# Six u blocks made from x before the norm, three side by side, with 1/rms multiplied on in their eviction

## The chip, the cores and the metric

The kernel runs on one core of one Trainium2 chip. The metric is device time in microseconds, the median of several runs. The engines are named as in the profile: PE (TensorE, matmuls; PEld are its weight loads), DVE (VectorE), ACT (ScalarE), POOL (GpSimd) and SP (SyncE, which here only issues DMAs). Each engine works through its own list of instructions in order, and waits for the others by semaphores.

## The reference, cut to what matters

T = 512 tokens, model width D = 1024. The program is one mixer block followed by two layers of another block; the change touches only the start of the mixer block.

```python
h = rms_norm(x, g_norm[l])                # x / sqrt(mean(x*x) + 1e-6) * g
z = h @ w_in[l]
q, k, v, fl, gf, u, gs, qm, gm, gl = split_cols(z)
log_f = log_sigmoid(fl + b_forget[l])     # 12 heads
y_fox = forgetting_attention(q, k, v, log_f)
y_s5 = s5_ssm(u, lam_re, lam_im, log_step, b_re, ...)   # u is 512 x 768
```

Since 1/rms is one number per token, `(x*g/rms) @ W` equals `((x*g) @ W)/rms`, the factor being put on column by column of the product.

## The kernel before

Activations lie feature by token: x is eight tiles of 128x512, `x[0]` to `x[7]`. A float32 matmul is made of three passes on values split in two, a high part and the rest: `mm3` (L115) issues `wh` by `h` (L117), `wh` by `l` (L118) and `wl` by `h` (L119). So each activation tile is split into h (ACT, L222) and l (DVE, L230), and each strip of weights (128x1024, 512 KB) is fetched by an SP DMA (`fetch`, L72 to L78), cast to `wh` on ACT (L93) and its rest `wl` made by DVE or, for each odd strip, by POOL (L96). A strip is two tiles of 128x512 and holds the weights of one block of 128 output features. `get` (L99) splits strips some time ahead of their use and fetches further ones.

The order of instructions on each engine is made at build time by the scheduler of the framework, from data dependences, a priority, and the kernel's own hints: `add_manual_dep` with `AFTER` (L44) orders an instruction behind another for the scheduler alone; on the chip there is no wait for it.

`block1` (L1473) begins: x comes in sixteen half tiles, ACT squares them and DVE sums the squares (`sq_acc`, L183 and L184). `norm` and `head` (L573) work by halves of the tokens: the sum over features on PE (`sumcols`, L190), mean and eps on DVE (`nv`, L208), the power -1/2 on POOL (`nr`, L210), the broadcast by PE (`bcast`, L197); then per tile `hu` = x times g times 1/rms on DVE (L562), its cast h on ACT and its rest l on DVE. With that, `head` makes the first two of six u blocks by halves (128x256, L593, L594, L597: first the passes with h, then those with l). Four more blocks come as a strip (L117 to L119). `upost` (L1497) evicts each block: an ACT copy with permuted columns to `us` (L1500), a DMA to a buffer `ud`, and four DMAs back as `u4` for the S5 stage. PSUM holds three buffers of the kind `mm` that blocks go to in turn.

Beside the head lie three things that nobody needs at once. `s5_setup` (L1124) makes the constants of the S5 stage: some hundred DVE steps on tiles of 128x24, among them two exponentials (`exact_exp`, L1091), with an ACT sine in between. `forget_load` makes the padded weights `flh` and `fll` of the forget projection (POOL memsets, L1350 and L1351, then an ACT cast and a DVE difference). `load16` and `s5_load` issue DMAs of constants. Behind the u blocks PE does the forget projection (24 matmuls of 512 columns, `pmm` from `h` and `flh`) and then fv, the v product of the forgetting attention (96 matmuls of 256 columns, L133 to L135), then its q and k.

Of the kernel before, what the change touches and what calls it, by code (L numbers as in the profile page):

```python
# [9 lines left out]
F32 = mybir.dt.float32  # L10
F32R = mybir.dt.float32r
BF16 = mybir.dt.bfloat16
I32 = mybir.dt.int32
AF = mybir.ActivationFunctionType
ALU = mybir.AluOpType
# [3 lines left out]
D = 1024  # L19
# [4 lines left out]
def f32(t):  # L24
    return t.bitcast(F32)
# [1043 lines left out]
class Blk1(Blk2):  # L1069
# [21 lines left out]
    def exact_exp(self, out, x):  # L1091

        k, r, q = self.small(), self.small(), self.small()
        xc = self.small()
        self.ts(xc, x, -150.0, 88.7, ALU.max, ALU.min)
        self.ts(k, xc, 1.4426950408889634, MAGIC)
        self.nc.vector.tensor_scalar(out=k, in0=k, scalar1=-MAGIC, scalar2=None, op0=ALU.add)
        self.stt(r, k, -0.693359375, xc, ALU.mult, ALU.add)
        self.stt(r, k, 2.12194440054690583e-4, r, ALU.mult, ALU.add)
        c = [1.0 / math.factorial(i) for i in range(9)]  # L1100
        self.nc.vector.tensor_scalar(out=q, in0=r, scalar1=c[8], scalar2=None, op0=ALU.mult)
        for i in range(7, 0, -1):
            self.stt(q, q, c[i], r, ALU.add, ALU.mult)
        self.nc.vector.tensor_scalar(out=q, in0=q, scalar1=1.0, scalar2=None, op0=ALU.add)
        ka, kb = self.small(), self.small()
        self.ts(ka, k, -126.0, 127.0, ALU.max, ALU.min)
        self.tt(kb, k, ka, ALU.subtract)
        for kk in (ka, kb):
            b = self.small(I32)
            self.ts(b, kk, 127.0, 8388608.0, ALU.add, ALU.mult)  # L1110
            self.tt(q, q, b.bitcast(F32), ALU.mult)
        self.nc.vector.tensor_copy(out, q)
# [360 lines left out]
    def block1(self):  # L1473
        nc, b = self.nc, self.base
        cst = self.t(b, [128, 1], F32, "hpi")
        nc.vector.memset(cst, 1.5707963267948966)
        self.halfpi = cst
        self.bmh = self.t(b, [128, 24], F32, "bmh")
        nc.vector.tensor_scalar(out=self.bmh, in0=self.col("b_merge", 0, 24), scalar1=0.5, scalar2=None, op0=ALU.mult)
        self.bgh = self.t(b, [128, 6], F32, "bgh")  # L1480
        nc.vector.tensor_scalar(out=self.bgh, in0=self.col("b_glu", 0, 6), scalar1=0.5, scalar2=None, op0=ALU.mult)
        x = [self.u(name="x") for _ in range(8)]
        with self.tc.high_priority():
            for hf in range(2):
                for j in range(8):
                    if 8 * hf + j == self.F0:
                        self.fetch(0)
                    nc.sync.dma_start(out=self.half(x[j], hf), in_=self.half(self.a["x"][:, j, :], hf))
        for hf in range(2):
            for j in range(8):  # L1490
                self.sq_acc(self.half(x[j], hf), j, slice(256 * hf, 256 * hf + 256))
        h = self.new_h()
        norm = self.norm(x, self.col("g_norm", 0, 8), None, h)
        u = [None] * 6
        self.y5 = [None] * 6

        def upost(j):  # L1497
            def f(pm):
                t = self.u(name="us")
                nc.scalar.copy(t.rearrange("p (i b) -> p b i", i=4), pm.rearrange("p (b i) -> p b i", i=4))  # L1500
                nc.sync.dma_start(out=self.ud[j], in_=t)
                u[j] = self.u(name="u4")
                for i in range(4):
                    nc.sync.dma_start(out=u[j][32 * i:32 * i + 32].rearrange("p (q b) -> p q b", q=4),
                                      in_=self.ud[j].rearrange("(q c) (i b) -> i c q b", q=4, i=4)[i])
            return f
        self.head(["u"] * 2, h, [upost(j) for j in range(2)],
                  norm, self.half, True)
        del x, norm
        fl = self.forget_load()  # L1510
        self.s5_load()
        self.load16()
        self.merge(self.strip("u", h, 8, [upost(j) for j in range(2, 6)]), [])
        merged = []
        ge, ges = [], ([], [])
        hm = self.fox(h, u, ge, ges, merged, fl)
        self.memory(h, hm, merged)
        return self.s5_out(h, ge, ges, merged)
# [535 lines left out]
```

## Time and profile before

| what | value |
|---|---|
| median of 3 runs | 2462.0 us (2461.26 to 2466.11) |
| profiled execution, its own time | 2459.34 us |
| its span in the trace | 2457.6 us |
| PE / DVE / ACT / POOL busy | 94% / 63% / 43% / 36% |
| DMA | 265.37 MB, mean 108 GB/s |

The span is the time from the first to the last instruction of the profiled execution; 1.7 us lie around it. A busy share is an average over stages with different limits, so the rows of the head below are read by stretch and engine. In a row of a timeline, the bracket at the end tells how long the engine was idle ahead of it and what ended that.

### The profile page before, as it was taken

The numbers are of one execution on the slowest core, as the hardware profiler recorded it, in microseconds if no ns is written. First come the engines' busy times: TensorE is split into PE (matmuls) and PEld (weight loads), VectorE is DVE, ScalarE is ACT, GpSimd is POOL, SyncE is SP. The second block draws the span as 40 slices with busy tenths as digits, with TensorE's granted clock in tenths as the row PEclk, the third lists the DMA queues.
The fourth block names the chain that finished last, engine by engine and source line by source line (L and its number), as shares of the span: only waits on it lengthen the run. The fifth ranks groups of instructions, "written<-read, shape, count | busy, mean of one in ns | idle before, by whom it ended". The sixth has DMA issues, their size and how long they took to land.

```text
span 2457.6 us, 33152 instructions
## 1 busy us (share of the span) xinstructions
PE 2322.2 (94%) x12138; PEld 1938.8 (79%) x12138; DVE 1538.6 (63%) x2573; ACT 1064.0 (43%) x1995; POOL 887.5 (36%) x810
## 2 busy tenths in 40 slices
PE   6999989989999889998999999998999899999999
PEld 5877768877888767787888888897778788888888
DVE  7567787657899788658278674257874746422222
ACT  4345543443333336643444324343565344533422
POOL 2445446635222264225132223126531523123212
PEclk9999999999999999999999999998999999999999
DMA  4311123312676321122137563232212224223222
GB/s 158 104 44 52 56 75 101 112 43 84 233 270 226 124 83 43 60 77 79 61 129 259 201 217 120 77 138 73 77 36 69 77 69 138 71 101 112 89 92 86
DMA packets 105620, 265.37 MB, mean 108 GB/s; under 512 B 13664, under 2 KB 23408, under 8 KB 105456
## 3 DMA queue, kind: packets, MB, share of 16 engines
q1 hardware_dynamic: 104304, 261.47, 31.5%
q8 instruction: 96, 1.57, 0.3%
q10 hardware_dynamic: 1152, 1.77, 0.2%
q14 instruction: 68, 0.56, 0.1%
HBM read 244.69 MB, written 9.44 MB: 103 GB/s over the span
## 4 chain that ended last, share of the span: by engine, by line
PE 63%; DVE 11%; issue 4%; ACT 3%; POOL 2%; DMA 1%; SPq 1%; DVEq 0%; POOLq 0%; ACTq 0%
PE pmm L117 17%; PE pmm L118 17%; PE pmm L119 17%; PE ps L320 3%; DVE wl L96 1%; DVE adacc L514 1%; DMA xs<-xg 1%; PE ppv L411 1%; PE ppv L410 1%; PE ppv L409 1%; DVE l L232 1%; PE pmm L134 1%; PE pmm L135 1%; PE pmm L133 1%; DVE xs L636 1%
## 5 line engine op out<-in xcount | busy, mean ns | idle before, releaser
L96 POOL TENSOR_TENSOR wl<-wr,wh 128x512 fp32r<-128x512 f32 x346 | 480.8, 1409 | 1122.6 <-ACT wh L93 968.0
L117 PE MATMUL pmm<-h,wh 128*128 128x512 f32 (+1 forms) x2112 | 824.1, 391 | 5.7 <-ACT wh L93 3.2
L119 PE MATMUL pmm<-h,wl 128*128 128x512 f32 (+1 forms) x2112 | 821.2, 389 | 2.1 <-POOL wl L96 1.8
L118 PE MATMUL pmm<-l,wh 128*128 128x512 f32 (+1 forms) x2112 | 819.5, 388 | 0.0
L119 PEld LDWEIGHTS pmm<-h,wl 128*128 128x128 f32 x2112 | 399.1, 189 | 85.7 <-POOL wl L96 4.3
L117 PEld LDWEIGHTS pmm<-h,wh 128*128 128x128 f32 x2112 | 399.4, 189 | 84.7 <-ACT wh L93 4.7
L118 PEld LDWEIGHTS pmm<-l,wh 128*128 128x128 f32 x2112 | 399.6, 189 | 77.3 <-DVE l L230 0.4
L93 ACT CAST wh<-wr 128x512 fp32r<-128x512 f32 (+1 forms) x692 | 385.1, 610 | 136.8 <-DMA wr<-in_w 118.8
L96 DVE TENSOR_TENSOR wl<-wr,wh 128x512 fp32r<-128x512 f32 x346 | 278.8, 836 | 30.3 <-ACT wh L93 26.9
L392 DVE TENSOR_TENSOR pl<-pe,ph 128x512 fp32r<-128x512 f32 (+4 forms) x168 | 121.4, 731 | 149.8 <-ACT ph L390 144.7
L230 DVE TENSOR_TENSOR l<-r,h 128x512 fp32r<-128x512 f32 x64 | 46.5, 726 | 220.9 <-ACT h L222 216.8
L971 DVE SCALAR_TENSOR_TENSOR x<-pmm,ada,x 128x512 f32<-128x512 f32 (+1 forms) x88 | 59.9, 682 | 180.5 <-PE pmm L119 180.0
L320 PE MATMUL ps<-qk,qk 128*128 128x512 f32 (+4 forms) x416 | 142.9, 381 | 24.6 <-POOL qk L683 7.4
L514 DVE SCALAR_TENSOR_TENSOR adacc<-adw,cact,adacc 128x512 f32<-128x512 f32 x168 | 156.5, 932 | 3.2
L994 ACT ACTIVATE r<-pmm 128x512 f32<-128x512 f32 x62 | 37.1, 598 | 257.1 <-PE pmm L119 257.1
L388 ACT ACTIVATE pe<-ps 128x512 f32<-128x512 f32 (+4 forms) x168 | 84.6, 503 | 102.8 <-PE ps L320 102.4
L320 PEld LDWEIGHTS ps<-qk,qk 128*128 128x128 f32 x416 | 81.0, 199 | 51.7 <-POOL qk L683 13.3
L117 PE MATMUL pmm<-yh,wh 128*128 128x512 f32 (+1 forms) x244 | 91.2, 377 | 5.8 <-ACT yh L1419 3.7
L632 POOL TENSOR_TENSOR qv<-qv,mhalf 128x8 f32<-128x8 f32 x34 | 62.9, 1852 | 86.6 <-DVE qv L631 83.1
L119 PE MATMUL pmm<-yh,wl 128*128 128x512 f32 (+1 forms) x244 | 90.7, 373 | 1.7 <-DVE wl L96 0.9
L390 ACT CAST ph<-pe 128x512 fp32r<-128x512 f32 (+4 forms) x168 | 88.8, 529 | 7.8 <-PE ppv L410 1.5
L118 PE MATMUL pmm<-yl,wh 128*128 128x512 f32 (+1 forms) x244 | 90.6, 372 | 0.3 <-DVE yl L1089 0.3
(386 smaller groups left out, 3993.2 us busy)
## 6 DMA issues: line engine op xcount, KB each, us to landing
wr<-in_w SPq DMA_DIRECT2D x324, 512.0 KB
adw<-in_wada SPq DMA_DIRECT2D x192, 256.0 KB
xs<-xg SPq DMA_DIRECT2D x136, 64.0 KB
wr<-in_w SPq DMA_DIRECT2D x22, 384.0 KB
xd<-x SPq DMA_DIRECT2D x16, 256.0 KB
x<-xd SPq DMA_DIRECT2D x16, 256.0 KB
x<-in_x SPq DMA_DIRECT2D x16, 128.0 KB
x<-in_x SPq DMA_DIRECT2D x8, 256.0 KB
```

The source lines that it names most:

```text
L93: ins = self.nc.scalar.copy(h[:, 0:m], r[:, c:c + m])
L96: eng.tensor_tensor(out=l[:, 0:m], in0=r[:, c:c + m], in1=f32(h)[:, 0:m], op=ALU.subtract)
L117: mm(out, wh, ah, start=start, stop=False)
L118: mm(out, wh, al, start=False, stop=False)
L119: self.pe = mm(out, wl, ah, start=False, stop=stop).ins.name
L320: mm(outs[i] if len(r.shape) == 2 else outs[i].rearrange("p (r i) -> p r i", r=r.shape[1]), w, r, start=first and i == 0, stop=last and i ...
L388: nc.scalar.activation(out=e[:, w], in_=pt[:, w], func=AF.Exp)
L390: nc.scalar.copy(ph[:, w], e[:, w])
L392: nc.vector.tensor_tensor(out=pl[:, w], in0=e[:, w], in1=f32(ph)[:, w], op=ALU.subtract)
L514: nc.vector.scalar_tensor_tensor(out=acc, in0=w, scalar=cc, in1=acc, op0=ALU.mult, op1=ALU.add)
L632: nc.gpsimd.tensor_tensor(out=v, in0=v, in1=self.mhalf, op=ALU.pow)
L971: nc.vector.scalar_tensor_tensor(out=x[j][:, s], in0=pm[:, s], scalar=ada[:, c + j:c + j + 1], in1=x[j][:, s], op0=ALU.mult, op1=ALU.add)
```

## The change

x now comes in eight whole tiles, with strips 0 to 2 between the first of them. For each tile ACT makes `rh` = x times g (L1495) and DVE the rest `rl` (line of `stt`, L1089); the squares are summed as before, whole tiles. Three u blocks are made side by side from `rh` and `rl`: for each of the eight tiles, nine matmuls. The sums of squares are turned to 1/rms inside the last tile's turn (`nv` on DVE, `nr` on POOL, L1527), the broadcast comes behind the third block, and ACT copies it to a tile `R` (L1528). The eviction `upost` is now a DVE product of the block and `R`, with permuted columns (`us`, by `tt`, L1086). Blocks four to six follow, also from `rh` and `rl`. The h tiles, which the rest of the mixer needs, are made from x, g and `R` (`hu` on DVE, h on ACT, l on DVE, whole tiles). The first step of each exponential of the S5 setup is ordered behind the last matmul of the fourth block. `forget_load`, `s5_load` and `load16` are called behind the u blocks as before.

```diff
-        self.ts(xc, x, -150.0, 88.7, ALU.max, ALU.min)
+        ins = self.nc.vector.tensor_scalar(out=xc, in0=x, scalar1=-150.0, scalar2=88.7, op0=ALU.max, op1=ALU.min)
+        self.tc.add_manual_dep(ins.ins, self.pe_u, self.AFTER, reason="setup")
...
+        g = self.col("g_norm", 0, 8)
+        raw = [], []
         with self.tc.high_priority():
-            for hf in range(2):
-                for j in range(8):
-                    if 8 * hf + j == self.F0:
-                        self.fetch(0)
-                    nc.sync.dma_start(out=self.half(x[j], hf), in_=self.half(self.a["x"][:, j, :], hf))
-        for hf in range(2):
             for j in range(8):
-                self.sq_acc(self.half(x[j], hf), j, slice(256 * hf, 256 * hf + 256))
+                if j < 3:
+                    self.fetch(j)
+                nc.sync.dma_start(out=x[j], in_=self.a["x"][:, j, :])
+        ws = []
+        for j in range(8):
+            hi, lo = self.u(F32R, "rh"), self.u(F32R, "rl")
+            nc.scalar.activation(out=hi, in_=x[j], func=AF.Copy, scale=g[:, j:j + 1])
+            self.stt(lo, x[j], g[:, j:j + 1], f32(hi), ALU.mult, ALU.subtract)
+            raw[0].append(hi)
+            raw[1].append(lo)
+            self.sq_acc(x[j], j)
+            if j < 3:
+                ws.append(self.get("u", 8))
         h = self.new_h()
-        norm = self.norm(x, self.col("g_norm", 0, 8), None, h)
...
+        R = self.u(name="R")
...
-                nc.scalar.copy(t.rearrange("p (i b) -> p b i", i=4), pm.rearrange("p (b i) -> p b i", i=4))
+                v = lambda z: z.rearrange("p (b i) -> p b i", i=4)
+                self.tt(t.rearrange("p (i b) -> p b i", i=4), v(pm), v(R), ALU.mult)
...
-        self.head(["u"] * 2, h, [upost(j) for j in range(2)],
-                  norm, self.half, True)
-        del x, norm
+        pms = [self.p("mm") for _ in range(3)]
+        pq = self.p("m")
+        for k in range(8):
+            for w, pm in zip(ws, pms):
+                self.mm3(pm, *w[k], raw[0][k], raw[1][k], k == 0, k == 7)
+            if k == 5:
+                self.sumcols(pq, self.sums["sacc"], [[128 * i] for i in range(4)])
+                v, r = (self.t(b, [128, 4], F32, n, 2) for n in ("nv", "nr"))
+                self.ts(v, pq[:, 0:4], 1.0 / D, 1e-6)
+                nc.gpsimd.tensor_tensor(out=r, in0=v, in1=self.mhalf[:, 0:4], op=ALU.pow)
+        nc.scalar.copy(R, self.bcast(r))
+        del ws
+        for j in range(3):
+            self.done(pms[j], upost(j))
+        it = self.strip("u", raw, 8, [upost(j) for j in range(3, 6)])
+        it[0]()
+        self.pe_u = self.pe
+        for j in range(8):
+            t = self.u(name="hu")
+            self.stt(t, x[j], g[:, j:j + 1], R, ALU.mult, ALU.mult)
+            self.hsplit(t, None, (h[0][j], h[1][j]))
+        self.merge(it[1:], [])
         fl = self.forget_load()
         self.s5_load()
         self.load16()
-        self.merge(self.strip("u", h, 8, [upost(j) for j in range(2, 6)]), [])
```

How the instructions stand on the engines, at the places that matter. In the rows a number behind a name is the buffer's; `x_111` to `x_118` are the tiles of x.

On ACT, after the change, while x comes in (`wr_125` is strip 2, `wr_163` strip 3, `wr_165` strip 4):

```order
L93 CAST wh_155<-wr_125 128x512
L93 CAST wh_159<-wr_125 128x512
L1495 ACTIVATE rh_169<-x_112,cols_69 128x512
L183 ACTIVATE sq_173<-x_112 128x512
L93 CAST wh_176<-wr_163 128x512
L93 CAST wh_180<-wr_163 128x512
L1495 ACTIVATE rh_186<-x_113,cols_69 128x512
L183 ACTIVATE sq_190<-x_113 128x512
L93 CAST wh_193<-wr_165 128x512
L93 CAST wh_197<-wr_165 128x512
```

The casts of strips 3 and 4 stand ahead of the tiles 2 and 3 of x; before, ACT had no casts of strips until h was nearly made.

On SP, after the change, the DMAs behind the eight x tiles (`wfl` to `c` are constants):

```order
L1490 DMA x_118<-in_x 128x512
L1344 DMA wfl_530<-in_wfl 128x96
L1346 DMA bfg_532<-in_bfg 128x48
L1118 DMA s5par_546<-in_s5p 128x72
L1123 DMA trow_556<-in_trow 128x128
L2007 DMA c_3_68<-in_c 128x2048
L78 DMA wr_163<-in_w 128x1024
```

Strip 3 is issued behind the constants, as it was before.

On DVE, after the change, the end of the first stretch of setup steps (`us_404` is the fourth block) and the start of h:

```order
L1086 TENSOR_TENSOR us_404<-pmm_379,R_254 128x128x4
L1113 COPY s5keep_883<-s5t_917 128x24
L1089 SCALAR_TENSOR_TENSOR s5t_955<-s5keep_883,s5t_955 128x24
...
L1086 TENSOR_TENSOR s5keep_883<-s5keep_883 128x24
L1089 SCALAR_TENSOR_TENSOR hu_412<-x_111,cols_69,R_254 128x512
...
L1086 TENSOR_TENSOR s5f_976<-s5f_976,s5t_971 128x24
L230 TENSOR_TENSOR l_246<-hu_412,h_238 128x512
L1089 SCALAR_TENSOR_TENSOR hu_416<-x_112,cols_69,R_254 128x512
```

and before, the same work around h (`hu` by halves; the first setup steps between them):

```order
L562 SCALAR_TENSOR_TENSOR hu_219<-x_114,cols_69,ps_207 128x256
L1083 TENSOR_SCALAR s5t_961<-s5par_448 128x24
L562 SCALAR_TENSOR_TENSOR hu_222<-x_115,cols_69,ps_207 128x256
L1083 TENSOR_SCALAR s5t_958<-s5t_961 128x24
L562 SCALAR_TENSOR_TENSOR hu_225<-x_116,cols_69,ps_207 128x256
L1097 TENSOR_SCALAR s5t_958<-s5t_958 128x24
L562 SCALAR_TENSOR_TENSOR hu_210<-x_111,cols_69,ps_285 128x256
```

After the change 74 setup steps stand between the first `us` and the first `hu`, and 25 more among the `hu` and `l`; every `hu` stands behind the l of the tile ahead of it. Before, all sixteen halves of `hu` stood ahead of the l and of all but a few of the steps.

On POOL, after the change (`wl_488` and `wl_492` are strip 7):

```order
L96 TENSOR_TENSOR wl_370<-wr_167,wh_369 128x512
L96 TENSOR_TENSOR wl_374<-wr_167,wh_373 128x512
L96 TENSOR_TENSOR wl_488<-wr_201,wh_487 128x512
L96 TENSOR_TENSOR wl_492<-wr_201,wh_491 128x512
L1351 MEMSET flh_534 128x512
L1352 MEMSET fll_535 128x512
```

and before (`wl_269`, `wl_273` are strip 3, `wl_505` strip 5):

```order
L96 TENSOR_TENSOR wl_269<-wr_262,wh_268 128x512
L96 TENSOR_TENSOR wl_273<-wr_262,wh_272 128x512
L1350 MEMSET flh_436 128x512
L1351 MEMSET fll_437 128x512
L1350 MEMSET flh_442 128x512
L1351 MEMSET fll_443 128x512
L96 TENSOR_TENSOR wl_505<-wr_266,wh_504 128x512
```

The memsets of `flh` moved from ahead of strip 5's splits to behind strip 7's. On ACT the casts of strips 6 and 7, between the last h and the cast of `flh`:

```order
L222 CAST h_245<-hu_440 128x512
L93 CAST wh_444<-wr_184 128x512
L93 CAST wh_448<-wr_184 128x512
L93 CAST wh_487<-wr_201 128x512
L93 CAST wh_491<-wr_201 128x512
L1353 CAST flh_534<-wfl_530 128x4x12
```

All eight h now stand ahead of those casts. On PE, after the change, from the end of the sixth block:

```order
L118 MATMUL pmm_497<-rl_232,wh_373 128x512
L119 MATMUL pmm_497<-rh_231,wl_374 128x512
L117 MATMUL pmm_559<-h_238,flh_534 128x512
L118 MATMUL pmm_559<-l_246,flh_534 128x512
L133 MATMUL pmm_606<-wh_444,h_238 128x256
```

The first forget matmul (`pmm_559`) follows the last u block at once, and fv is interleaved with the rest of them; before, the forget matmuls stood among those of the sixth block.

## Rows read from the trace of the kernel before

**Rows 1.** The page, part 1: busy us, share of the span, instructions of each engine.

```profile
PE 2322.2 (94%) x12138; PEld 1938.8 (79%) x12138; DVE 1538.6 (63%) x2573; ACT 1064.0 (43%) x1995; POOL 887.5 (36%) x810
```

**Rows 2.** Table by stretches; columns as its head line says (us from the start).

```profile
0.00:5.00 5.00, 0.00 (x0) 0.00 (x0) 2.30 (x16) 2.24 (x5) 1.19 (x6) 1.00 0.53 156
5.00:10.00 5.00, 0.00 (x0) 0.00 (x0) 2.60 (x7) 3.60 (x10) 0.00 (x0) 1.00 0.92 275
10.00:15.00 5.00, 2.24 (x8) 1.86 (x8) 2.70 (x9) 1.58 (x5) 0.71 (x1) 1.00 1.00 352
15.00:20.00 5.00, 2.24 (x8) 1.85 (x8) 4.39 (x16) 3.48 (x9) 0.70 (x1) 1.00 0.40 132
30.00:35.00 5.00, 1.01 (x5) 0.97 (x6) 4.86 (x13) 0.00 (x0) 3.37 (x5) 0.95 0.65 205
35.00:40.00 5.00, 5.00 (x32) 5.00 (x32) 4.93 (x22) 0.00 (x0) 0.00 (x0) 0.71 0.03 8
```

**Rows 3.** Timeline of PE: start us, us, operation and tiles, idle before and releaser.

```profile
33.99 0.38 PE L597 MATMUL ppv<-l,wh 128*128 128x256 f32 x1 [4.01 <-DVE l L230]
...
49.09 0.39 PE L117 MATMUL pmm<-h,wh 128*128 128x512 f32 x1
...
53.62 0.39 PE L119 MATMUL pmm<-h,wl 128*128 128x512 f32 x1
...
70.27 0.28 PE L133 MATMUL pmm<-wh,h 128*128 128x256 f32 x1
...
72.67 0.28 PE L135 MATMUL pmm<-wh,l 128*128 128x256 f32 x1
...
76.03 0.60 PE L1369 MATMUL ps<-c,zr 128*128 128x128 f32 x4
```

**Rows 4.** Timeline of ACT, as in rows 3.

```profile
27.79 1.14 ACT L93 CAST wh<-wr 128x512 fp32r<-128x512 f32 x2 [1.82 <-DMA wr<-in_w]
...
46.37 0.35 ACT L1352 CAST flh<-wfl 128x48 fp32r<-128x48 f32 x2
...
66.85 1.09 ACT L1500 COPY us<-pmm 128x512 f32<-128x512 f32 x1 [5.22 <-PE pmm L119]
70.47 0.59 ACT L1365 COPY zr<-pmm 128x512 f32<-128x512 f32 x1 [2.54 <-PE pmm L119]
...
82.41 0.37 ACT L770 CAST v<-pmm 128x256 fp32r<-128x256 f32 x1 [3.25 <-PE pmm L135]
```

**Rows 5.** Groups by form (busy us, mean ns); of line L1086 (ns min/median/max).

```profile
L230 DVE TENSOR_TENSOR l<-r,h 128x512 fp32r<-128x512 f32 x64 | 46.5, 726 | 220.9 <-ACT h L222 216.8 <-issue 3.6
...
L222 ACT CAST h<-r 128x512 fp32r<-128x512 f32 x64 | 39.8, 621 | 2.2
...
L1086 DVE TENSOR_TENSOR gw<-gw,s5y x6: 1040/1082/1095, 274.3 to 645.4; 128x512 f32<-128x512 f32 x6
```

**Rows 6.** Timeline of POOL, as in rows 3.

```profile
16.39 0.70 POOL L210 TENSOR_TENSOR nr<-nv,mhalf 128x2 f32<-128x2 f32 x1 [3.78 <-DVE nv L208]
...
31.40 0.52 POOL L1350 MEMSET flh<- 128x512 f32 x1
...
50.44 2.54 POOL L96 TENSOR_TENSOR wl<-wr,wh 128x512 fp32r<-128x512 f32 x2 [17.07 <-ACT wh L93]
```

**Rows 7.** Timeline of DVE, as in rows 3; s5t are the setup's small tiles.

```profile
24.54 3.17 DVE L1089 SCALAR_TENSOR_TENSOR s5t<-s5t,s5t 128x24 f32<-128x24 f32 x5
...
38.89 0.39 DVE L1089 SCALAR_TENSOR_TENSOR s5t<-s5t,s5t 128x24 f32<-128x24 f32 x2
...
42.21 0.17 DVE L1204 TENSOR_SCALAR s5keep<-s5keep 128x24 f32<-128x24 f32 x1
...
50.62 1.17 DVE L1086 TENSOR_TENSOR s5t<-s5pw 128x24 f32<-128x24 f32 x1
```

**Rows 8.** Waits of PE: us in total, times, longest.

```profile
PE ps L1321 <- DVE s5to L1317: 6.0, 2, 4.7
PE ps L1312 <- DVE s5b L1308: 5.6, 3, 3.0
```

## Prediction

> **What bounds the kernel now.** I read the page's busy shares first: TensorE is busy for 2322.2 of 2457.6 us [rows 1], so an edit counts by what it does to TensorE's idle time. Then the table by stretches [rows 2]: in the first 20 us TensorE has 4.48 us of work, while the DMA engines are full from 10 to 15 us (share 1.00) and then run dry. Then each engine's timeline of the head. TensorE starts blocks one and two, stops until 33.99 (it waited 4.01 us for a `l` of VectorE), and from there works without a gap through the forgetting attention's v product (fv, from 70.27) [rows 3]. That product ends when ScalarE's cast at 82.41 is let go [rows 4]. I count the head up to that **82.4 us**; behind it the program is the same but for small swaps.
>
> So before, TensorE idles early, because u waits for the norm; the S5 setup (some 100 steps of 128x24 on VectorE) is done beside TensorE's work and nobody waits for it. The change starts u earlier, but queues the setup, and the making of h, on VectorE between the norm and the first user of h.
>
> **Step 1, until 1/rms is there (R).** Up to 17 us the before moved 4.58 MB: 5 x (156+275+352+132) GB/s [rows 2]. Of the new order, strip 3 (0.52 MB) comes behind all of it, the big constants included, while ScalarE's casts of strip 3 stand ahead of tile 2's `rh`. 5.10 MB at 352 GB/s are 14.5 us; begun at 2.3 us (before's first 0.78 MB by 5 us, at that rate) this is 16.8. The other bound is before's own end plus a strip, 16.9 + 1.5 = 18.4. I take 17.5. Two casts (1.14 us [rows 4]) and the `rh` (0.62, as a cast [rows 5]) give 19.3: until then TensorE has only the 18 matmuls of tiles 0 and 1. The other 54 go at 0.2265 us (twenty steps from 49.09 to 53.62 [rows 3]): 12.2. After the stall the first go at the lower clock: before, after the stop that ends at 33.99, the granted clock is 0.95 in the stretch from 30 us and 0.71 in the one from 35 [rows 2], 5 x 0.05 + 5 x 0.29 = 1.7 us lost. The sums and the broadcast, four matmuls each, take 0.60 each (as at 76.03 [rows 3]); the power step (0.70 [rows 6]) lies beside the eight matmuls behind the sums. ScalarE's copy of R is a plain one, 0.59 [rows 4]. R: 19.3+12.2+1.7+1.2+0.6 = **35.0**.
>
> In a sentence by itself: the Trainium skill ("DMA: Bandwidth & Descriptors", section "Queues, rings and completion order") says that one issuer's descriptors are consumed in ring order on each DMA engine, which would leave strip 3 behind the constants as I have it; no row shows two transfers of this order apart.
>
> **Step 2, TensorE's u blocks.** The fourth needs the first one's PSUM buffer, so it waits for `us` 0, now on VectorE and strided. Such a product takes 1.08 there [rows 5], ScalarE's copy of that form 1.09 [rows 4]. It starts at 36.1; 72 matmuls are 16.3; TensorE ends the sixth at **52.4**, where before ended it at 66.6 (the copy at 66.85 [rows 4]). That is the gain, 14.2 us.
>
> **Step 3, VectorE from R to the last l.** Between R and the first `hu` stand four `us` (4.3 us) and 74 of the setup's small steps. Before, 30 such steps took 42.38 − 38.89 us, 0.116 each [rows 7]: 8.6. The splits of strip 5 run on GpSimd in that time (a pair is 2.54 us, as at 50.44 [rows 6]); beside such pairs one small step took 1.17 (50.62), and five took 3.17 (24.54) [rows 7]. The bounds are 0 (the pair falls beside the `us`) and 2.4; I take 1.2. First `hu` at 49.1. Then every row waits for the one ahead: `hu` on VectorE, h on ScalarE, l on VectorE, next `hu`. With 0.73 for l, the same for `hu` (the nearest row), 0.62 for h [rows 5], that is 2.08 eight times, 16.6. The 25 other small steps lie in the gaps while h is cast and cost nothing; the cover gone, they cost 2.9. Last l at **65.7**.
>
> On the collision the Trainium skill ("SBUF — State Buffer", section "SBUF: two separate sides") says that the port pair of VectorE and GpSimd is an exclusive lock, taken by VectorE operations with two SBUF inputs against a GpSimd operation that reads SBUF; the step of 1.17 agrees, and by it a `us` (one input from PSUM) is never held: the lower bound if the pair falls there, and an end 1.2 us sooner.
>
> **Step 4, from l to TensorE.** The forget projection stands first on TensorE; it needs `flh`, whose memset stands on GpSimd behind strip 7's splits, and these wait for ScalarE's casts of strips 6 and 7, now behind all eight h. Last h 65.0; three casts 1.7; the pair 2.54; memset 0.52 [rows 6]; cast of `flh` 0.2 (two in 0.35 [rows 4]): **70.0**. `us` 4 and 5, queued behind the last l and strip 6's splits on VectorE, free the next PSUM buffers at 68 and 69, just ahead. TensorE idles from 52.4 to 70.0.
>
> **Step 5.** Then 24 forget matmuls (5.4), 96 of fv at 0.12 (twenty from 70.27 to 72.67 [rows 3]; 11.5), the four transposes (0.6), and 1.7 for the low clock after the gap: 19.2. fv ends at 89.2, where before ended it at 82.4: **+6.8 us**. ScalarE loses six copies; that is free, it idles there. The SP queue takes `s5bc` behind the u transfers; its user in S5 is tens of us off, no cost. Behind the head TensorE's order is the same but for neighbours swapped. The S5 stage has 11.6 us of TensorE waits on VectorE [rows 8]; I take 0 for the swaps and half of these waits, 6 us either way, as the bound.
>
> The profiled execution took 2459.3 us, 1.7 more than its span, and the median of the runs is 2462.0, 2.7 above it. 2459.3 + 6.8 = 2466.1, against the median 2468.8: **2469**.
>
> **Bounds.** Low: strip 3 lands before ScalarE comes to it. Then TensorE is the limit: from about 8 us (x 0 and strip 0 landed and split), 72 x 0.2265 + 1.7 + 1.2 + 0.6 gives R at 28; setup at 0.10 a step and no collision, 11.7; chain 16.0; tail 4.2; step 5 19.2: 79.1, or −3.3 (2459). High: R 35.9, steps at 0.145, collision 2.4, chain 17.6, tail 4.5, 19.7 behind: 95.1, +12.7 (2475), with the swaps 2481.
>
> **Rivals.**
> - *Strip 3 is no stall* (the low bound of step 1 alone): R 28.0, 7 us off every later number: −0.2 us, **2462**, same. For it: the constants are issued just ahead of it and could finish after it. Against: even at full rate 5.10 MB need 14.5 us.
> - *The collisions and waits pile up*: the high bound, **2475 to 2481**. For it: step by step waits that before hid behind TensorE are now on the path.
> - *Faster*: the place is the S5 stage. u 0 to 5 leave TensorE 14 us earlier, and VectorE's setup is over before the stage. Should TensorE's 11.6 us of waits there for `s5b` and `s5to` vanish, the sum is 6.8 − 11.6 = −4.8, **2457**; it turns the sign once more than 6.8 of the 11.6 goes. Against: those waits end on products within the stage, which this order leaves alone. Also a setup that goes faster than 0.116 leads here, but 74 x 0.026 is only 1.9 us.
> - *The change doesn't do what it says*: the tie of the setup behind the fourth block is an order only, with no wait; 74 of its steps stand ahead of h all the same. This is in the sum.
>
> **How the numbers follow.** Forecast case 0.60 (2465 to 2475, a tail of 0.05 within the same), strip no stall 0.18, pile-up 0.13, faster 0.09. About 0.2% (4.9 us) is what a measurement can tell from no change. Slower: 0.55 + 0.13 + a little of the second = 0.69. Same: 0.05 + 0.16 = 0.21. Faster: 0.09 + 0.01 = 0.10. The range of 8 in 10 runs from the lower bound less the middle of the S5 waits' reach, 2457, to the high bound, 2482.
>
> **What would show it.** Right: a stall of ScalarE until about 17 us ahead of strip 3's casts; R copied at about 35; the sixth block over by 53; first `hu` at 49, last l at 66, TensorE idle for some 17 us before the forget matmuls, its clock low after. Wrong: R before 30 (step 1), small steps well under 0.1 us, a chain under 1.8 us a tile (step 3), or a gap under 10 us; then the kernel is even or faster. If the head comes out as summed and the total doesn't, the S5 stage took or gave it.

## The result, and the profile after

The changed kernel takes **2476.6 us** (median of 4 runs, 2474.3 to 2479.2), the kernel before 2462.9 on the same chip (4 runs, 2461.3 to 2466.1): a ratio of 1.0054 with a 95% interval of 1.0037 to 1.0072, so 9 to 18 us **slower**. Slower was forecast, at 2469 and within 2457 to 2482; the sign and the range held, the size was 7.6 us short. The profiled execution took 2477.1 us, its span is 2475.3 (before: 2457.6).

The head went as predicted, 0.8 to 2.3 us later from step to step. First TensorE's waits up to 100 us, then ScalarE's timeline (start us, us, operation and tiles, idle time before and what ended it), both of after:

```profile
PE pmm L117 <- ACT flh L1353: 18.3, 1, 18.3
PE pmm L117 <- ACT wh L93: 7.8, 1, 7.8
PE pmm L117 <- ACT rh L1495: 4.1, 1, 4.1
PE pmm L117 <- DVE us L1086: 1.8, 1, 1.8
```

```profile
17.32 1.14 ACT L93 CAST wh<-wr 128x512 fp32r<-128x512 f32 x2 [5.41 <-DMA wr<-in_w]
18.36 0.72 ACT L1495 ACTIVATE rh<-x,cols 128x512 fp32r<-128x512 f32 x1
...
35.16 0.59 ACT L1528 COPY R<-ps 128x512 f32<-128x512 f32 x1 [8.85 <-PE ps L197]
...
66.15 0.62 ACT L222 CAST h<-hu 128x512 fp32r<-128x512 f32 x1 [1.42 <-DVE hu L1089]
66.67 2.17 ACT L93 CAST wh<-wr 128x512 fp32r<-128x512 f32 x4
71.54 0.23 ACT L1353 CAST flh<-wfl 128x48 fp32r<-128x48 f32 x1 [2.70 <-POOL flh L1351]
```

ScalarE stood 5.41 us before strip 3's cast because the strip had not landed (TensorE's 4.1 us are the same stall), R came at 35.16, and the casts of strips 6 and 7 (66.67) stood behind the last h. VectorE's timeline of after shows why h was late:

```profile
35.77 1.06 DVE L1086 TENSOR_TENSOR us<-pmm,R 128x512 f32<-128x512 f32 x1 [3.32 <-ACT R L1528]
36.68 0.97 DVE L1095 TENSOR_SCALAR s5t<-s5par 128x24 f32<-128x24 f32 x1
37.69 1.21 DVE L1083 TENSOR_SCALAR s5t<-s5t 128x24 f32<-128x24 f32 x1
...
50.94 0.74 DVE L1089 SCALAR_TENSOR_TENSOR hu<-x,cols,R 128x512 f32<-128x512 f32 x1
...
66.80 0.69 DVE L230 TENSOR_TENSOR l<-hu,h 128x512 fp32r<-128x512 f32 x1 [0.68 <-ACT h L222]
...
85.08 0.44 DVE L1183 TENSOR_SCALAR s5bc<-s5bc 128x384 f32<-128x384 f32 x1 [11.93 <-DMA s5bc<-in_s5bc]
```

From R's first product (35.77) to the first `hu` (50.94) lie the setup's steps, then eight rounds of 2.03 to 2.17 us each (from one `hu` to the next), the last l ending at 67.49. The last row is a wait of 11.93 us for a transfer, `s5bc`; in the kernel before VectorE waited 2.74 us for it, at 57.56. It comes up again below. TensorE's timeline of after:

```profile
53.13 0.39 PE L119 MATMUL pmm<-rh,wl 128*128 128x512 f32 x1
71.83 0.79 PE L117 MATMUL pmm<-h,flh 128*128 128x512 f32 x1 [18.31 <-ACT flh L1353]
...
72.84 0.41 PE L133 MATMUL pmm<-wh,h 128*128 128x256 f32 x1
```

It ended the sixth u block at 53.5, 13 us ahead of before, and gave all of it away in one gap of 18.3 us. The first product of q and k (the step behind fv) starts at 91.50, in before at 82.21. Behind it the kernel lost another 8.4 us by these two profiles (17.7 in all), about 5 by the medians. The busy times of after, from the page's part 1, answer to [rows 1]:

```profile
PE 2330.0 (94%) x12090; PEld 1940.0 (78%) x12090; DVE 1538.4 (62%) x2563; ACT 1061.0 (43%) x1982; POOL 884.3 (36%) x809
```

TensorE is busy 7.8 us longer for the same work, so a part of the loss is not idle time at all. The mean granted clock is 0.973 against 0.981; the difference lies mostly in the first 100 us (0.88 against 0.98), where the gap is.

### The profile page after: what moved, and what is told of

It reads as the page before. It is cut to its first block, busy times and chain, and to the rows that moved or that the text cites. A ratio compares the mean times of both kernels' runs of the same rounds, so it can differ in the third digit from the quotient of the medians.

```text
span 2475.3 us, 33039 instructions
## 1 busy us (share of the span) xinstructions
PE 2330.0 (94%) x12090; PEld 1940.0 (78%) x12090; DVE 1538.4 (62%) x2563; ACT 1061.0 (43%) x1982; POOL 884.3 (36%) x809
## 4 chain that ended last, share of the span: by engine, by line
PE 70%; DVE 14%; issue 6%; ACT 4%; POOL 4%; DMA 2%; SPq 0%; DVEq 0%; POOLq 0%; ACTq 0%
PE pmm L117 18%; PE pmm L119 18%; PE pmm L118 18%; PE ps L320 4%; DVE adacc L514 1%; DVE wl L96 1%; PE pmm L134 1%; PE ppv L411 1%; PE ppv L409 1%; PE ppv L410 1%; PE pmm L135 1%; PE pmm L133 1%; DVE rs L439 1%; DVE unm L345 1%; POOL wl L96 1%
## 5 line engine op out<-in xcount | busy, mean ns | idle before, releaser
L117 PE MATMUL pmm<-h,wh 128*128 128x512 f32 (+1 forms) x2080 | 813.7, 392 | 6.2 <-ACT wh L93 3.2
L119 PE MATMUL pmm<-h,wl 128*128 128x512 f32 (+1 forms) x2080 | 809.6, 390 | 3.4 <-POOL wl L96 3.1
L118 PE MATMUL pmm<-l,wh 128*128 128x512 f32 (+1 forms) x2080 | 808.5, 389 | 0.0
L119 PEld LDWEIGHTS pmm<-h,wl 128*128 128x128 f32 x2080 | 393.8, 189 | 85.7 <-POOL wl L96 5.2
L117 PEld LDWEIGHTS pmm<-h,wh 128*128 128x128 f32 x2080 | 393.9, 190 | 83.8 <-ACT wh L93 4.1
L118 PEld LDWEIGHTS pmm<-l,wh 128*128 128x128 f32 x2080 | 394.4, 190 | 76.6 <-DVE l L230 0.4
```

The costliest lines, as they stand in the source:

```text
L117: mm(out, wh, ah, start=start, stop=False)
L118: mm(out, wh, al, start=False, stop=False)
L119: self.pe = mm(out, wl, ah, start=False, stop=stop).ins.name
```

## The experiments

The theory **Q** is the prediction's: u is early, but the setup and the alternation of `hu`, h and l stand on VectorE between R and the first user of h, and `flh` behind them. **S** is its step 1: R is late because strip 3 stalls ScalarE. Rivals: **G**, it is the low clock behind the gap that costs; **N**, taking a gap away only brings the next wait; **D**, the loss behind the head is of another kind than the loss in it.

All medians are set against before's median on the same chip. Two profiles of before start the q and k product at 82.21 and 83.29, mean 82.75; "first score" is ScalarE's first exponential of an attention score, at 120.58 and 121.7, mean 121.1. Both columns give the distance from those means; two profiles of one kernel lie up to 1.1 us apart in them.

| kernel | median us | above before | ratio, 95% | copy of R starts | last l | gap of TensorE | q and k | first score |
|---|---|---|---|---|---|---|---|---|
| after | 2476.6 | 13.7 | 1.0037–1.0072 | 35.2 | 67.5 | 18.3 | +8.8 | +8.7 |
| setup behind block 6 | 2472.4 | 11.0 | 1.0032–1.0065 | 36.6 | 62.2 | 13.7 | +6.8 | +7.6 |
| `hu` in place | 2469.5 | 8.0 | 1.0019–1.0046 | 35.2 | 62.0 | 10.2 | +3.4 | +4.2 |
| strip 3 later | 2467.6 | 6.2 | 1.0013–1.0036 | 29.4 | 60.0 | 16.4 | +1.1 | +1.8 |
| forget tiles early | 2472.8 | 11.4 | 1.003–1.0063 | 35.3 | 67.6 | filled | +0.9 | +9.1 |
| gap filled | 2472.6 | 10.2 | 1.0026–1.0053 | 35.9 | 68.3 | filled | +7.4 | +8.2 |
| forget and s5bc early | 2470.2 | 7.8 | 1.0022–1.0047 | 36.5 | 68.9 | filled | +2.5 | +6.5 |
| three mends | 2464.5 | 2.1 | 1.0–1.0019 | 28.8 | 59.4 | 1.3 | −6.5 | 0.0 |
| all mends | 2465.4 | 2.9 | 1.0002–1.0024 | 29.0 | 55.0 | 6.3 | −8.1 | −3.4 |
| tie undone | 2473.6 | 13.2 | 1.0033–1.0065 | 38.7 | 66.5 | 10.8 | +7.0 | +7.8 |
| before, delayed | 2473.1 | 11.7 | 1.0032–1.0059 | – | 39.4 | none | +9.7 | +9.7 |

Only the gap-filling edit leaves the queues of VectorE, ScalarE and GpSimd as in after. With each of the other edits of after the scheduler also moves rows behind the head, so that behind the first score these kernels differ by more than their edit.

**The setup behind the sixth block.**

```diff
         it[0]()
-        self.pe_u = self.pe
...
         self.merge(it[1:], [])
+        self.pe_u = self.pe
```

> The changed kernel with one part of the change moved further: the S5 setup's tie is to the last matmul of the sixth u block, not of the fourth. VectorE then has the four us at R (35.2) and, behind the fourth, hu; the setup's steps lie among the hu and l. Theory Q (VectorE's queue between R and l is what makes TensorE wait): us 3 waits for the fourth block until about 42.4, first hu near 43.5 where it was 50.9; with 6 to 9 small steps in each gap of 0.7 us a tile takes 2.2 to 2.5 us, last l at 62 to 63.5 (was 67.5), TensorE restarts 4.3 later, q and k product at 86 to 88 (was 91.5): 4 to 6 us less in all. Theory S (the stall of ScalarE on strip 3 sets the head): no change, within 1 us. Theory D (the loss lies behind the head): no change.

R came 1.4 us later and first `hu` at 45.57; the small steps went into the gaps at 2.04 to 2.14 us a tile, as free as the prediction's 25 were. Last l came 5.3 us earlier and the gap shrank from 18.3 to 13.7, but the q and k product came only 1.9 earlier. From the last l to TensorE's restart at 68.70 it was 6.5 us instead of 4.3, since the casts of strips 6 and 7 now lay between the setup's steps on ScalarE and GpSimd's pair took 3.00 us; a wait of 1.1 us for `fll` followed. For Q in direction, short of its size (4 to 6).

**`hu` written in place.**

```diff
         for j in range(8):
-            t = self.u(name="hu")
+            t = x[j]
```

> The changed kernel with hu written over x instead of into a fresh tile of the ring. All eight hu then stand right behind the first us, and ScalarE's eight casts follow without VectorE between; the l still stand behind the setup's steps. Theory Q: hu done at about 42, h at 43, but the first l only when three us and some 74 steps are through, 54 to 55; eight l and 15 steps, last l at 61 to 62.5; q and k product at 85 to 87, 5 to 6 us less than 91.5. So the alternation hu, h, l costs about 5, the setup ahead of it the rest. Theory S: no change. Theory D: no change.

VectorE, ScalarE and GpSimd of this kernel, same columns:

```profile
36.67 7.16 DVE L1089 SCALAR_TENSOR_TENSOR x<-x,cols,R 128x512 f32<-128x512 f32 x8
...
59.35 1.28 DVE L230 TENSOR_TENSOR l<-x,h 128x512 fp32r<-128x512 f32 x2
```

```profile
53.14 0.22 ACT L1155 ACTIVATE s5t<-s5t 128x24 f32<-128x24 f32 x1 [16.37 <-DVE s5t L1083]
...
55.01 4.24 ACT L222 CAST h<-x 128x512 fp32r<-128x512 f32 x8
```

```profile
60.89 4.66 POOL L96 TENSOR_TENSOR wl<-wr,wh 128x512 fp32r<-128x512 f32 x2 [21.58 <-ACT wh L93]
```

Eight `hu` now take 7.16 us in one piece, eight h 4.24, and the l follow from 55.87 to 62.02, where after's rounds of the three took 16.55: it was the ring of buffers that made each `hu` wait for the l ahead. Last l is only 5.5 us earlier, since the setup's steps on ScalarE (53.14), which wait for VectorE's, stand ahead of h there: h was done at 59.25, where 43 was expected. The q and k product is 5.4 us earlier than in after. R is untouched (35.15). Part of the gain goes back at once: GpSimd's pair beside the l took 4.66 us against 2.54 [rows 6].

**Strip 3 later.** The first three blocks' splits alone stand ahead of the norm.

```diff
+        self.NW = 3, 1
         ws = []
         for j in range(8):
...
+        self.NW = 3, 3
         h = self.new_h()
```

> The changed kernel with get splitting only the strip that it hands out while x comes in (3 ahead again afterwards), so that no cast of strips 3 and 4 stands ahead of tiles 2 and 3 on ScalarE. Theory S: R at 28 to 29 instead of 35.2, and as everything behind waits for R, the q and k product 6 to 7 us earlier, 84.5 to 85.5, the total as much less. Theory Q alone, with an R that matters little since the setup fills the time: the q and k product moves by under 2. A rival: casts of strips 3 to 5 now stand behind R and the fourth block waits for them, which gives 2 to 3 of the 7 back.

R at 29.43 instead of 35.16, the q and k product 7.7 us earlier, TensorE's 4.1 us wait gone. ScalarE's rows:

```profile
17.98 0.62 ACT L183 ACTIVATE sq<-x 128x512 f32<-128x512 f32 x1
29.43 0.58 ACT L1530 COPY R<-ps 128x512 f32<-128x512 f32 x1 [10.83 <-PE ps L197]
29.92 3.22 ACT L93 CAST wh<-wr 128x512 fp32r<-128x512 f32 x6
```

The last of the norm's squares ends at 18.6 against 26.3; strip 3's casts moved behind R and hold nobody up. S stands: at the first score this was worth more than any other single edit (6.9 us). In the median too (6.2 above before, against 8.0 with `hu` in place), but those intervals overlap.

**The forget tiles early.** Memsets and casts of `flh` stand ahead of the u blocks.

```diff
         R = self.u(name="R")
+        fl = self.forget_load()
...
-        fl = self.forget_load()
         self.s5_load()
```

> The changed kernel with forget_load called ahead of the u blocks, so that GpSimd's memsets of flh stand ahead of strip 5's splits. The forget matmuls then wait for h and l of their tile alone and lie in TensorE's gap. Theory Q: last l unchanged at 67.5, but TensorE has the 24 forget matmuls done by then and a gap in pieces; fv from about 68.5; q and k product at 81.5 to 83.5, 8 to 9.5 us less than 91.5. If the gap's low clock has its own price, a good part of 1.7 us of it goes too. Theory D: the total moves by clearly less than the head.

The 18.3 us gap is gone: TensorE now follows the h in pieces, the longest wait on them 0.6. The q and k product comes 7.9 us earlier than in after. And at the first score nothing of it is left: +9.1 against +8.7. VectorE and TensorE of this kernel show a part of where it went:

```profile
87.64 0.36 DVE L1183 TENSOR_SCALAR s5bc<-s5bc 128x384 f32<-128x384 f32 x1 [15.32 <-DMA s5bc<-in_s5bc]
```

```profile
91.07 0.47 PE L117 MATMUL pmm<-h,wh 128*128 128x512 f32 x1 [1.82 <-DVE v L771]
```

VectorE stood for 15.32 us on `s5bc`, with the forget gates and the splits of v behind it. The transfer is issued at 81.39, since SP had first to wait for `us` 4 and 5 and store u. The prediction had written "no cost" beside this transfer; in after it holds VectorE for 11.93 us too, only TensorE is still busy with fv then.

**The gap filled.** 78 extra matmuls on TensorE between the sixth block and the forget projection, their product thrown away; nothing else moved.

```diff
         self.merge(it[1:], [])
+        pd = self.p('s')
+        for k in range(78):
+            ins = nc.tensor.matmul(pd, raw[0][k % 8][:, 0:128], raw[0][k % 8], start=k == 0, stop=k == 77)
+            self.tc.add_manual_dep(ins.ins, self.pe, self.AFTER, reason='fill')
```

> The changed kernel with 78 extra matmuls of 512 columns on TensorE between the sixth u block and the first forget matmul (78 x 0.2268 is 17.7 us, the gap from 53.4 to 71.8); their product is thrown away. The queues of the other engines are word for word those of the changed kernel, so only TensorE's activity in the gap differs. Theory C (the gap costs more than its length, since TensorE restarts at the lower clock): the first forget matmul still at 71.8 to 72.2, but the 20 matmuls behind it at full pitch, 2.6 us instead of the 4.6 they took (71.83 to 76.47); q and k product at 89.3 to 89.7 instead of 91.5; total 2 us less. If the low clock were no matter of the gap, 91.5 again. Theory D (what is lost behind the head, some 4 to 8 us, comes from the gap as well): total 4 or more less.

A table by stretches of after and then of this kernel (us from:to and length, busy us and count of PE, PEld, DVE, ACT, POOL, granted clock, DMA share, GB/s):

```profile
65.00:70.00 5.00, 0.00 (x0) 0.00 (x0) 4.32 (x7) 2.69 (x5) 1.60 (x2) 0.50 0.05 11
70.00:75.00 5.00, 3.17 (x13) 2.98 (x14) 0.95 (x3) 0.46 (x2) 2.90 (x5) 0.50 0.49 179
75.00:80.00 5.00, 5.00 (x23) 4.39 (x23) 0.00 (x0) 0.00 (x0) 0.00 (x0) 0.83 0.77 229
```

```profile
65.00:70.00 5.00, 5.00 (x24) 4.14 (x23) 3.77 (x6) 3.22 (x6) 0.80 (x1) 1.00 0.00 0
70.00:75.00 5.00, 4.25 (x26) 3.50 (x25) 1.87 (x4) 0.46 (x2) 3.76 (x6) 1.00 0.49 162
75.00:80.00 5.00, 5.00 (x25) 4.20 (x24) 0.00 (x0) 0.00 (x0) 0.00 (x0) 1.00 0.78 231
```

With TensorE kept busy the clock stays at its upper level (2.4 GHz), where after works at the lower one (1.2, shown as 0.50) until 76.47. The restart's first 19 matmuls take 4.64 us in after (71.83 to 76.47) and 2.59 here (72.68 to 75.27): **2.0 us** is what the low clock costs in the head. G is real and small there. The q and k product came at 90.19, 1.3 earlier, since R was 0.7 later in this profile (35.89).

Behind the head this kernel says more. Its other engines' queues are after's, row for row, yet its profile takes 2378.0 us from the q and k product to the end, where both profiles of after take 2383.8 and those of before 2375.4 and 2376.9. By the medians the kernel is 3.5 us closer to before than after is, between the numbers of C (2) and D (4 or more), and the intervals overlap; so whether the gap also costs something behind the head stays open.

**Forget tiles and `s5bc` early**: the edit above, and `self.s5_load()` moved up behind it.

> e4 with s5_load called early too, so that the four s5bc transfers stand on SP ahead of the u transfers. In e4 VectorE stood still for 15.3 us until 87.6, its scale of s5bc being queued ahead of the v evictions and the forget steps, and e4 had given back its 8 us by the first score. Theory N (the s5bc transfers moved behind the u transfers are the next wait in line): VectorE is free there, the first score's exponential at 121 plus 1 to 3 us where e4 had 130.6 (121 plus 9.6), the total 5 to 8 us under e4, near 2466. If something else held it: within 1.5 us of e4.

VectorE's 15 us wait is gone, and TensorE's 1.82 us wait for v with it. At the first score +6.5 against +9.1, with R 1.2 us later in this profile; the median is 3.6 lower against before. N is right about the place and had put the price (5 to 8) too high. The other 4 us between the q and k product (+2.5) and the first score stay unexplained.

**Three mends**: strip 3 later, forget tiles early, `s5bc` early. Then **all mends**: those, `hu` in place, and the setup tied behind block 6.

> e3, e4 and the early s5_load together: strips split one at a time while x comes in, forget weights and s5bc early; the setup stays where the change put it. Theory Q plus S plus N: R at 29.4 as in e3, last l at 60 as in e3, forget matmuls in the gap as in e4, so q and k product at 75.5 to 77 where before had 82.2; total, with the 4 us that every variant so far lost behind the head, 2457 to 2461, even with before (2461.4) or a little better.

> e7 with hu written over x (e2) and the setup tied behind the sixth u block (e1) as well. Theory Q: h and l are whole before the sixth u block ends, so TensorE has no gap at all; q and k product at 71 to 73, 9 to 11 under before. Total 2452 to 2458 if what lies behind the head stays as in the others; if the setup, now run late, is itself wanted by the S5 stage, some of it comes back: 2458 to 2463.

Neither beats the kernel before, though their heads are 6 and 8 us ahead of it at the q and k product; both were expected level with it or faster. All mends has a new gap, where none was expected: its eight `hu` (9.23 us in all, from 30.52) stand ahead of the second and third `us`, and TensorE waits 6.3 us, until 40.85, for a PSUM buffer. With three mends the lead is gone at the first score. Stretches of before, then of three mends, and its longest wait there:

```profile
105.00:110.00 5.00, 5.00 (x36) 4.15 (x35) 4.84 (x10) 2.32 (x4) 4.32 (x5) 1.00 0.35 110
110.00:115.00 5.00, 5.00 (x44) 4.96 (x44) 4.79 (x14) 1.92 (x3) 4.78 (x7) 1.00 0.31 105
```

```profile
105.00:110.00 5.00, 3.59 (x29) 3.27 (x28) 4.84 (x12) 2.12 (x4) 4.47 (x6) 1.00 0.14 20
110.00:115.00 5.00, 3.47 (x19) 3.48 (x20) 4.88 (x7) 0.63 (x2) 4.42 (x6) 0.66 0.24 89
```

```profile
111.53 0.61 PE L277 MATMUL ps<-c,mcm 128*128 128x128 bf16 x4 [2.94 <-DVE mcm L271]
```

VectorE (4.8 of 5 us) and GpSimd (4.4) are as full as in before, but now TensorE has run out of work beside them (3.5 of 5) and loses its clock (0.66). By these rows VectorE bounds that stage, and an earlier TensorE only waits there; before had just enough TensorE work to cover it.

**The tie undone**: the order behind the fourth block, which the change adds, taken back.

```diff
-        ins = self.nc.vector.tensor_scalar(out=xc, in0=x, scalar1=-150.0, scalar2=88.7, op0=ALU.max, op1=ALU.min)
-        self.tc.add_manual_dep(ins.ins, self.pe_u, self.AFTER, reason="setup")
+        self.ts(xc, x, -150.0, 88.7, ALU.max, ALU.min)
```

> The changed kernel with the tie of the S5 setup taken back, so that one part of the change is undone and the rest kept. The scheduler then puts the setup's steps among rl and the sums and ahead of nv; four us and the eight hu and l follow R with nothing between. Theory Q: some 40 steps stand between the last sum and nv, so R is 3 to 4 us later, 38.5 to 39.5; hu waits for the fourth block's us, 47; eight tiles at 2.08 us, last l at 63.5 to 64.5; TensorE restarts at 68 where it was 71.8, q and k product at 87.5 to 88.5, the total 3 to 4 us under the changed kernel's. If the tie spared TensorE something, the total is over the changed kernel's 2476.6.

The setup now runs ahead of R and delays R by 3.6 us (38.74), as expected; last l comes only 1.0 us earlier than in after, where 3 to 4 were expected. VectorE shows why:

```profile
49.19 1.10 DVE L1086 TENSOR_TENSOR us<-pmm,R 128x512 f32<-128x512 f32 x1 [6.02 <-PE pmm L119]
50.12 0.71 DVE L1089 SCALAR_TENSOR_TENSOR hu<-x,cols,R 128x512 f32<-128x512 f32 x1
```

The first `hu` is still queued behind the product of the fourth block, and VectorE stood idle for 6.02 us until TensorE had that block done. So with the setup out of the way the fourth block bounds the chain of h, at almost the same time. The q and k product gains 1.7, the median is level with after within its interval.

**After and before once more**, one execution each.

> The changed kernel once more, for a second profile. Theory D1 (what its first profile lost behind the head, 8.4 us by the spans of two profiled runs, comes from the swapped rows): the first score at 121 plus 9 to 10 again and the end at plus 16 to 18 against the first profile of before. Theory D2 (most of it is the spread of the granted clock from run to run): the same head, within 0.7 us, but an end that differs by 2 us or more, with the mean granted clock moving along, about 1 us for 0.001.

> The kernel before once more, for a second profile. Theory D2: the head within 0.7 us (q and k product at 82.2), the span above the first profile's 2457.6 by 2 to 4 us, since the runs' median is 2462, with a granted clock under 0.981. Theory D1: a span within 1 us of 2457.6.

2477.3 and 2462.0 us; spans of 2475.5 and 2460.2. Both repeat: from the q and k product to the end the profiles of after take 2383.8 us both times, those of before 2375.4 and 2376.9. So 7 to 8 us behind the head is not one odd profile. After's second profile came as D1 has it; before's second is 2.6 us over its first, as D2 has it, and 1.1 of that arose in the head.

**The kernel before, delayed.** 40 extra matmuls behind the u blocks, product thrown away; but for three rows that change places with a neighbour all queues keep before's order.

```diff
         self.merge(self.strip("u", h, 8, [upost(j) for j in range(2, 6)]), [])
+        pd = self.p('s')
+        for k in range(40):
+            ins = nc.tensor.matmul(pd, h[0][k % 8][:, 0:128], h[0][k % 8], start=k == 0, stop=k == 39)
+            self.tc.add_manual_dep(ins.ins, self.pe, self.AFTER, reason='fill')
```

> The kernel before with 40 extra matmuls of 512 columns on TensorE behind the u blocks and ahead of the rest of the forget projection (40 x 0.2265 = 9.1 us of added work whose product is thrown away). All engines keep the order of rows of before but for one neighbour swapped on TensorE and two on VectorE. So this head is as late as the changed kernel's (9.3 us at the q and k product), without the changed kernel's order behind the head. Theory D1 (the loss behind the head comes from the rows that the changed kernel swaps there): the q and k product 9 us later than in before, the same 9 us at 284 us and at the end: a median 9 us above the kernel before, within 2. Theory T (the loss behind the head comes from the delay itself, since transfers and the other engines then meet TensorE's work at other moments, or the clock is granted otherwise): the offset grows from 9 us at the head to 14 to 18 at the end, and the median is 14 to 17 us above the kernel before.

The delay is +9.7 at the q and k product and at the first score, and 11.7 at the median, between the two theories' numbers: 2.0 us of it arise behind the head, 3 to 4 by the profiled execution (2472.2 − 92.5 = 2379.7 us against 2375.4 and 2376.9). Its median's interval reaches from 7.9 to 14.5, so a loss behind the head is likely here, not shown. From the q and k product to the end, over the same number of matmuls, in before, after, before delayed and the kernel with the gap filled:

```profile
82.20:2457.60 2375.40, 2262.84 (x11808) 1885.62 (x11806) 1488.97 (x2383) 1028.85 (x1923) 866.87 (x779) 0.98 0.31 106
91.49:2475.30 2383.81, 2270.69 (x11808) 1891.03 (x11806) 1483.73 (x2390) 1028.77 (x1923) 863.86 (x779) 0.98 0.31 106
92.48:2472.20 2379.72, 2263.74 (x11808) 1885.01 (x11806) 1493.36 (x2383) 1028.36 (x1923) 864.45 (x779) 0.98 0.32 106
90.18:2468.20 2378.02, 2262.85 (x11808) 1886.02 (x11806) 1491.64 (x2396) 1031.13 (x1927) 863.44 (x779) 0.98 0.32 106
```

After's TensorE is busy 7.9 us longer there, in its second profile 4.1 (2266.93) with the same end; the delayed kernel's only 0.9. Counted matmul by matmul, both profiles of after lose 3.4 and 3.5 us between 284 and 319 us of before's time, and have lost 5.4 and 5.5 at 510. From 284 to 510 us, before and the same matmuls of after:

```profile
284.00:510.00 226.00, 211.06 (x1126) 178.82 (x1125) 164.13 (x239) 98.36 (x192) 125.02 (x122) 0.97 0.26 87
292.95:524.75 231.80, 214.38 (x1126) 179.92 (x1125) 161.26 (x241) 98.99 (x194) 126.30 (x122) 0.96 0.26 86
```

It begins with two waits of TensorE that before does not have. They lie beside the S5 stage's copies to `s5bt`, where rows changed places. The rows are of TensorE in after, then of ScalarE in before and in after.

```profile
314.58 1.16 PE L1269 MATMUL ps<-u,s5bt 128*128 128x128 f32 x8 [1.40 <-ACT s5bt L1260]
...
317.32 0.39 PE L409 MATMUL ppv<-ph,v 128*128 128x256 f32 x1 [1.28 <-ACT ph L390]
```

```profile
298.70 1.07 ACT L1259 COPY s5bt<-ps 128x512 f32<-128x512 f32 x2
```

```profile
310.93 0.57 ACT L1260 COPY s5bt<-ps 128x512 f32<-128x512 f32 x1
...
313.97 0.56 ACT L1260 COPY s5bt<-ps 128x512 f32<-128x512 f32 x1
```

In before both copies to `s5bt` are done 2.9 us ahead of their first use on TensorE (302.69). In after the second copy ends at 314.53, at the end of a chain on ScalarE that had waited 7.97 us for GpSimd, and TensorE waits for it. Six kernels of the table have these rows in after's order (after, setup behind block 6, strip 3 later, gap filled, all mends, tie undone), and all six wait there, 0.69 to 1.41 us for `s5bt` and 1.27 or 1.28 for `ph`. The other five have before's order and neither wait. From the first score to the end the six lose 2.0 to 6.3 us by the table, 4.4 in the mean, the five 1.3 to 3.8, 2.3 in the mean.

So the swapped rows cost something: 2.7 us of waits at this place are shown. How much of it reaches the end is not: the kernel with the gap filled has the same two waits, and its loss at the end is small. Whether the rest comes from the delay, from the clock or from the spread of the runs can't be told either, since the medians' intervals are 3 to 4 us wide on either side.

## Why the prediction was right or wrong, point by point

- **What counts is TensorE's idle time, and the gap moves rather than goes**: right. Predicted idle from 52.4 to 70.0, found from 53.5 to 71.83, ended by `flh` as said.
- **Step 1**, R done at 35.0: done at 35.75 (35.16 + 0.59). The strip's landing was put at 17.5 and its cast started at 17.32; the experiment that moved the strip shows the stall as the cause. The rival "strip 3 is no stall" falls. Of the 0.75 us that it failed by, 0.70 are the sums and the broadcast: eight matmuls each, not four, they took 0.81 and 1.09 us where the sum had 0.60 each (rows below). The power step (1.01 instead of 0.70) ended beside the matmuls that cover it.
- **Step 2**: fourth block predicted at 36.1, found at 36.89 (the same 0.8); end of the sixth 52.4 against 53.5.
- **Step 3**: from R to the first `hu` 14.1 were predicted and 15.2 found (35.75 to 50.94). The collision held two steps, 0.97 and 1.21 long with a usual pitch of 0.116, some 2.0 us instead of the 1.2 taken; a wait of 0.30 us for ScalarE's sine step, which the sum did not have, is the rest. Two more errors cancel: the four `us` held VectorE for 0.92 us each and not 1.08, and the other 72 small steps came every 0.124 us and not every 0.116. The chain: 16.6 predicted, 16.55 found. That small steps in its gaps are free was shown twice, here and where the whole setup went into them.
- **The exclusive pair of ports**, which the Trainium skill ("SBUF — State Buffer", section "SBUF: two separate sides") ties to VectorE operations in a 2-port perf mode or with two SBUF inputs: the prediction took the second half alone. The step held longest here, 1.21 at 37.69, beside GpSimd's pair of 2.53 us from 36.34, has one tensor input. By this trace the collision is wider than the prediction read it; in which mode the step ran no run shows.
- **Step 4**: 4.3 us for the tail from the last l, predicted and found (67.49 to 71.83).
- **Step 5**: 19.2 predicted, 19.7 found (91.50 − 71.83). The low clock was put at 1.7 and measured at 2.0. The end of fv was forecast at 89.2, and the product that follows it started at 91.50: the head's sum failed by 2.3 us, 0.75 in step 1, 1.1 in step 3 and 0.5 here. Against before the product is 9.3 us later, where 6.8 was forecast.
- **"`s5bc` … no cost"**: right for this kernel, wrong as a reason. VectorE waits 11.93 us for it, hidden by fv; once the gap ahead is taken away, TensorE waits for what stands behind it.
- **The step that failed: "I take 0 for the swaps"** behind the head. Measured: 5 us by the medians, 7 to 8 by the profiles, where 6 was given as the bound. The place named, the S5 stage, is right for a part: at the first score (+8.7) nothing is lost yet, but two waits of 1.40 and 1.28 us near 315 us, the first of them for that stage's `s5bt`, are new and go with the swapped rows, which are some tens on VectorE and not a few neighbours. The rest, most of it longer busy time of TensorE, has no cause shown. That the total still lies within the range given is owed to the allowance of 6 us, not to the sum.
- **Rival "faster"** (S5's waits vanish because VectorE is free earlier): in part. The waits for `s5b` and `s5to` [rows 8] fell from 11.6 to 8.3 us, but those for VectorE's `pl` (split scores of the attention) rose from 3.5 to 9.3, so nothing was won.
- **Rival "pile-up", 2475 to 2481**: the total lies in it, but not for its reason; its terms for the head (95.1) did not come.

The sums and the broadcast on TensorE in after, and the power step on GpSimd, beside the row of 128x2 in [rows 6]:

```profile
31.31 0.95 PE L190 MATMUL ps<-c,sacc 128*128 128x1 f32 x8
...
34.07 1.05 PE L197 MATMUL ps<-c,nr 128*128 128x128 f32 x8
```

```profile
32.54 1.01 POOL L1527 TENSOR_TENSOR nr<-nv,mhalf 128x4 f32<-128x4 f32 x1 [11.54 <-DVE nv L1083]
```

## What to carry to other kernels

Before work is moved ahead of a wait, list what then stands between that wait and the next user on every in-order queue: here the block products came 13 us earlier, and small steps, buffer reuse, casts and memsets on three other engines then left TensorE idle for 18. A first mend shows the next bound only when the time is read at a later milestone: one edit gave 7.9 us at one and nothing at the next. And do not put the rows that change places behind a head at nothing: here they brought 2.7 us of new waits, 220 us after the head.

## What was not expected of the hardware

- A 128x24 `tensor_scalar` on VectorE with one tensor input took 1.21 us beside a GpSimd pair, ten times its usual pitch; and GpSimd's own pair took 4.66 us beside VectorE's l, against 2.54 [rows 6].
- GpSimd's power step on 128x4 took 1.01 us, on 128x2 0.70 [rows 6].
- TensorE's granted clock, behind an idle time of 18.3 us, stayed at 0.50 for the first 4.6 us of work; with the idle time filled it was 1.00 in the same stretch.
- Two executions of one kernel, after, took 2383.8 us each behind the head for the same 11808 matmuls, and yet TensorE was busy for 2270.69 us in one and 2266.93 in the other; in before it was 2262.84 and 2262.20. What decides this stays open.
